# Projections of q, k, v and u interleaved, mean-square matmul issued later, and the state-space output moved to a pool of its own

## The chip, the cores and the metric

One core of a Trainium2 chip runs the kernel. The metric is device time in microseconds (us). The engines are TensorE (PE in the profile; PEld is its loading of stationary operands), VectorE (DVE), ScalarE (ACT), GpSimd (POOL) and SyncE (SP), which issues every DMA of this kernel from one queue in order. Each engine runs its own instructions strictly in the order in which they stand in its queue, and waits at an instruction whose inputs or whose destination are not ready.

## The reference, cut to what matters

One layer over 2048 tokens of 1024 features, all in float32. One projection of the normed input gives q, k, v, two SiLU gates, the state-space input u and the merge logits. Attention is differential (two softmaxes, the second weighed with -lambda), the second branch is a diagonal complex state space with GELU and a gated linear unit, and both are merged and projected out.

```python
h = rms_norm(x, norm_gain[layer])
z = h @ w_in[layer]
q, k, v, gate_a, u_s, gate_s, merge_logits = jnp.split(z, IN_SPLITS, axis=-1)
q = rms_norm(q.reshape(B, L, ATTN_HEADS, 2, ATTN_SUB_DIM), q_norm_gain[layer])
k = rms_norm(k.reshape(B, L, ATTN_HEADS, 2, ATTN_SUB_DIM), k_norm_gain[layer])
o_a = diff_attention(q, k, v, lam, rel_bias_table, diff_subln_gain[layer], lam_init)
o_a = o_a * jax.nn.silu(gate_a)
o_s = s5_branch(u_s, ...)          # y = Re(C x) + D u, x_t = lambda x_(t-1) + B u_t; GELU; GLU
o_s = o_s * jax.nn.silu(gate_s)
g = jax.nn.sigmoid((merge_logits + merge_gate_b[layer]).astype(f32)).astype(x.dtype)
merged = g_a * (o_a @ proj_attn[layer]) + g_s * (o_s @ proj_ssm[layer])
x = x + merged @ w_out[layer]
```

## The kernel before

**Precision.** Each float32 operand is split into an upper half (`hh`, `wh`, `uh`) and the rest (`hl`, `wl`). A product takes three matmuls, upper by upper, upper by lower and lower by upper (`split3`, L42 to L46). The copy that makes the upper half runs on ACT (`hilo`, L840 to L844), the subtraction on POOL or DVE.

**Stages.** The tokens are worked in four blocks of 512 (`NTB`, `TB`). `phase1` (L101) projects the normed input. `load_x` brings a block of x, scales and splits it into `hh[t]`, `hl[t]`, and computes the tokens' mean square. The weights come in groups of 256 columns (`load_w`) or tiles of 128 (`load_w1`), and are split as they arrive.

- `qk` (L207) makes 256 columns of q or k for 512 tokens: two halves of 24 matmuls each into PSUM tiles `ps_qk`, ACT squares them, DVE adds the squares. The norm is left pending: `later()` runs it (`qk_norm`, L229) behind the first half of the next block. It begins with two matmuls `ms` against a block matrix of ones (L231, L232). DVE and ACT then turn the mean square into a factor (`newton`, L90), DVE scales both halves, and each is split into `qh` and `ql` and stored to DRAM in four DMAs. `qh` and `ql` share the tag `"o"` with two buffers.
- `value` (L247) makes 256 columns of v for 128 tokens in 24 matmuls of 256 columns. Behind v's blocks 2 and 3 of a token block it also calls `later()`.
- u takes four tiles of 128 columns (L293 to L316), then come 24 tiles of gate columns (`gate`), SiLU for eight and tanh for sixteen.

The order in the program is: q group 0 with v group 4 behind each token block, then q group 1 alone, v group 5 alone, k groups 2 and 3 alone, u, then the steps of `mid()`, and the gates. The last 512 tokens of the last two gate columns (`LATE = 2`) are left to `last()`.

`mid()` holds the state space's work of small matrices and the constants of attention. `ssm_prep` (L706) computes the discretized matrices with tiny operations on DVE. In a loop of four rounds POOL makes `cp` (C times powers of lambda, L785 to L796, stored to the DRAM tensor `CD`), DVE makes `wn` and PE transposes it (`ps_w`, L810). `ssm_states` scans the chunks on DVE. `ssm_out` (L915) computes the output in 16 groups: load u, the states `x`, the matrices `w` and the Toeplitz tile `tm`, split all four, 12 matmuls of 256 columns into `ps_y`, and a GELU through ACT (Square), POOL, DVE, ACT (Tanh) and DVE.

`early()` loads the first head's K, V and Q and takes the PSUM banks for scores. Attention then runs over four heads and 16 blocks of 128 queries each: scores `ps_s` (L528, L529), maxima, exponentials and the combination of both halves on DVE and ACT, transposes `ps_t` (L560), values `ps_o` (L568). The gated linear unit (`ps_g`), the state space's projection and, at the end, the output projections (`Tail`) fill in beside it.

**What sets the order.** The program is written as one sequence. A scheduler places each instruction on its engine's queue at build time, by the order of the program and a timeline that it keeps of engines and buffers, so steps that are far apart in the text can be interleaved on an engine. Buffers come from pools in SBUF and PSUM; a pool that takes the place of a closed one waits until the instructions that used that place are done.

## Time and profile before

| | |
|---|---|
| time, median of 3 runs | 1815.27 us (1812.55 to 1816.9) |
| span of the profiled execution | 1807.6 us (7.7 us less than the median time) |
| busy share of the span | PE 94%, PEld 79%, DVE 55%, ACT 38%, POOL 18% |
| mean granted clock of TensorE | 0.979 |
| DMA | 239.06 MB, mean 132 GB/s |

The stages follow each other on PE like this, from the first and last starts of their matmuls in the trace's answers by tile:

| stage | from the span's start, us |
|---|---|
| projections of q, k and v, up to the last mean square | 7.3 to 375.6 |
| u | 358.6 to 456.6 |
| transposes of the state-space matrices (`ps_w`) | 456.6 to 509.9 |
| gates, up to the late ones; the state space's output (`ps_y`) 877.4 to 1024.9 among them | 512 to 1060.8 |
| scores and values of attention; the gated linear unit and the state space's projection among them | 1046.2 to 1576.0 |
| output projection | 1553.3 to 1800.7 |

How to read it: PE is the engine with the largest busy share, but the share is a mean over stages. In a row of idle time, the name behind the arrow is what the engine waited for. A row of a timeline gives the start, the duration, engine, line, operation, what is written and read, and in brackets the wait ahead of it. A matmul's duration in such a row includes its way through the array; the rate is read from the distance between two starts. A row of a table of stretches gives, behind the stretch's length, the busy time and the count of instructions of PE, PEld, DVE, ACT and POOL, the granted clock (1.00 is full speed), the share of the DMA engines' time and the rate.

### The profile page before, as it was taken

To read this page: it belongs to the slowest core of one execution; us is meant where nothing else is said; L and a number is where in the kernel's file an instruction comes from. 1 tells how busy PE (TensorE), PEld (TensorE's weight loads), DVE (VectorE), ACT (ScalarE), POOL (GpSimd) and SP (SyncE) were. 2 spreads that over 40 slices of the span, in tenths; PEclk is the share of its full clock that TensorE was granted. 3 is DMA by queue.
4 is the path that set the end of the run, shared out by engine and by line. 5 is a ranking of instruction groups with operands and counts; after the bars stand their busy time and mean duration, and the time that the engine had idled before them with its cause. 6 is when DMAs were issued, how large, how long until landed. Compare 5 with 4: busy or idle time off the path is not lost.

```text
span 1807.6 us, 24838 instructions
## 1 busy us (share of the span) xinstructions
PE 1701.5 (94%) x8720; PEld 1432.4 (79%) x8720; DVE 997.1 (55%) x2400; ACT 682.3 (38%) x1404; POOL 328.1 (18%) x442
## 2 busy tenths in 40 slices
PE   7879798889699999999999999999999999999999
PEld 5777786677588887887888878878888879888887
DVE  7644314469832495495223277678677678643331
ACT  5443222220123413311344366667554567511100
POOL 4331110004200000000345334553011022100000
PEclk9989899999899999999999999999999999999999
DMA  5332322233444323225656584763554543554532
GB/s 168 102 100 87 92 73 72 69 105 84 126 139 121 122 76 122 80 71 158 185 153 169 171 262 116 198 212 112 193 178 133 161 139 117 186 156 151 148 100 82
DMA packets 213005, 239.06 MB, mean 132 GB/s; under 512 B 41456, under 2 KB 151440, under 8 KB 211856
## 3 DMA queue, kind: packets, MB, share of 16 engines
q1 hardware_dynamic: 212880, 237.47, 43.5%
q8 instruction: 69, 1.13, 0.3%
q14 instruction: 56, 0.46, 0.1%
HBM read 146.44 MB, written 90.96 MB: 131 GB/s over the span
## 4 chain that ended last, share of the span: by engine, by line
PE 58%; DMA 17%; DVE 16%; ACT 3%; issue 3%; POOL 1%; SPq 1%; DVEq 0%; ACTq 0%; POOLq 0%
PE ps_p L44 8%; PE ps_p L45 8%; PE ps_p L46 8%; DMA K<-ql 5%; PE ps_o L568 5%; DVE t L879 4%; DMA Q<-ql 4%; PE ps_o L45 3%; PE ps_o L46 3%; PE ps_o L44 3%; PE ps_s L528 3%; PE ps_s L529 3%; PE ps_t L560 2%; DVE V L879 2%; PE ps_a L46 2%
## 5 line engine op out<-in xcount | busy, mean ns | idle before, releaser
L44 PE MATMUL ps_p<-hh,w 128*128 128x512 f32 x896 | 353.6, 395 | 2.4 <-DVE u L313 1.2
L45 PE MATMUL ps_p<-hl,w 128*128 128x512 f32 x896 | 353.2, 394 | 0.0
L46 PE MATMUL ps_p<-hh,w 128*128 128x512 f32 x896 | 352.7, 394 | 0.0
L44 PEld LDWEIGHTS ps_p<-hh,w 128*128 128x128 f32 x896 | 170.5, 190 | 38.0 <-DVE q L240 2.0
L46 PEld LDWEIGHTS ps_p<-hh,w 128*128 128x128 f32 x896 | 170.4, 190 | 35.3 <-issue 0.7
L45 PEld LDWEIGHTS ps_p<-hl,w 128*128 128x128 f32 x896 | 170.4, 190 | 34.5 <-issue 0.7
L541 ACT ACTIVATE e<-e,mm 128x640 f32<-128x640 f32 (+11 forms) x96 | 136.2, 1419 | 63.8 <-DVE mm L539 62.9
L568 PE MATMUL ps_o<-V,at 128*128 128x128 f32 x1088 | 148.5, 276 | 2.3 <-ACT sq L574 1.8
L568 PEld LDWEIGHTS ps_o<-V,at 128*128 128x128 f32 x1088 | 141.4, 192 | 9.3 <-ACT sq L574 2.3
L329 DVE TENSOR_TENSOR z<-ps_p,E 128x512 f32<-128x512 f32 x96 | 65.9, 686 | 132.7 <-PE ps_p L46 132.7
L531 DVE TENSOR_SCALAR_CACHE_REDUCE e<-ps_s 128x512 f32<-128x512 f32 (+1 forms) x192 | 120.6, 640 | 31.2 <-PE ps_s L529 29.7
L528 PE MATMUL ps_s<-K,Q 128*128 128x512 f32 (+3 forms) x320 | 129.0, 405 | 1.1 <-DVE e L531 0.8
L529 PE MATMUL ps_s<-K,Q 128*128 128x512 f32 (+3 forms) x320 | 115.9, 365 | 0.0
L44 PE MATMUL ps_qk<-hh,wh 128*128 128x512 f32 x256 | 101.6, 403 | 12.6 <-DVE wh L138 7.7
L45 PE MATMUL ps_qk<-hl,wh 128*128 128x512 f32 x256 | 101.2, 399 | 1.4 <-DVE hl L175 1.4
L46 PE MATMUL ps_qk<-hh,wl 128*128 128x512 f32 x256 | 101.9, 398 | 0.3 <-DVE wl L141 0.3
L335 ACT ACTIVATE z<-z,hmb 128x512 f32<-128x512 f32 x64 | 46.3, 723 | 144.6 <-DVE z L329 131.0
L560 PE MATMUL ps_t<-ident,e 128*128 128x128 f32 x544 | 85.1, 274 | 4.6 <-ACT at L562 2.5
L551 DVE SCALAR_TENSOR_TENSOR e<-e,cf 128x128 f32<-128x128 f32 (+7 forms) x64 | 88.2, 1378 | 1.4
L562 ACT COPY at<-ps_t 128x512 f32<-128x512 f32 (+3 forms) x160 | 79.3, 522 | 18.4 <-PE ps_t L560 17.8
L560 PEld LDWEIGHTS ps_t<-ident,e 128*128 128x128 f32 x544 | 66.4, 141 | 16.6 <-ACT at L562 4.2
L534 DVE CUSTOM_DVE_ANT_0 e<-ps_s,nb 128x384 f32<-128x384 f32 (+3 forms) x128 | 70.1, 552 | 16.6 <-PE ps_s L529 15.5
(334 smaller groups left out, 3464.4 us busy)
## 6 DMA issues: line engine op xcount, KB each, us to landing
wraw<-win SPq DMA_DIRECT2D x80, 256.0 KB
TM<-z SPq DMA_DIRECT2D x30, 512.0 KB
t<-TM SPq DMA_DIRECT2D x40, 256.0 KB
xs<-xT SPq DMA_DIRECT2D x32, 256.0 KB
u<-US SPq DMA_DIRECT2D x64, 128.0 KB
K<-K SPq DMA_DIRECT2D x8, 1024.0 KB
Q<-Q SPq DMA_DIRECT2D x32, 256.0 KB
Q<-Q SPq DMA_DIRECT2D x64, 128.0 KB
```

The costliest lines, as they stand in the source:

```text
L44: nc.tensor.matmul(out, wh, xh, start=start, stop=False)
L45: nc.tensor.matmul(out, wh, xl, start=False, stop=False)
L46: nc.tensor.matmul(out, wl, xh, start=False, stop=stop)
L528: nc.tensor.matmul(ps, Q[:, 0, s, 128 * b:128 * b + 128], Kt[s][:, ks], start=True, stop=False)
L529: nc.tensor.matmul(ps, Q[:, 1, s, 128 * b:128 * b + 128], Kt[s][:, ks], start=False, stop=True)
L531: nc.vector.tensor_scalar(out=et[:, ks], in0=ps, scalar1=0.0, scalar2=3e38, op0=ALU.add, op1=ALU.min, accum_out=mc[:, i:i + 1])
L541: nc.scalar.activation(out=et, in_=et, func=AF.Exp, bias=mm, scale=-1.0, accum_out=su)
L551: nc.vector.scalar_tensor_tensor(out=e[0], in0=e[1], scalar=cf, in1=e[0], op0=ALU.mult, op1=ALU.add)
L560: nc.tensor.transpose(pt[:, x], e[:, o:o + 128], k.ident)
L562: nc.scalar.copy(AT[g][:, :w], pt[:, :w])
L568: nc.tensor.matmul(po, AT[x // 4][:, x % 4], Vt[x // 8][:, x % 8], start=x == 0, stop=x == n - 1)
L879: tt = lambda o, a, b, op: eng.tensor_tensor(out=o, in0=a, in1=b, op=op)
```

## The change

**Fillers.** `qk` now takes a function `between(i)` that it calls behind each half. In the q groups 0 and 1 it issues two blocks of `value`; in the k groups 2 and 3 it issues one u tile (`state`) behind each half of token blocks 0 to 2, and both of token block 3 behind that block's second half. So v group 5 moves from behind q group 1 into it, and the four u columns from behind k into it. `later()`, with the two `ms` matmuls, now stands behind the fillers of the first half, and v's blocks no longer call it.

**u.** It takes its norms from `RT`, four tiles of `newton` made ahead of k, is written time-reversed within a chunk of eight steps, and is stored in 16 DMAs of 256 KB rather than 8 of 512 KB. Its weights take two buffers each of the tags `wh` and `wl`, which the groups of 256 columns use as well.

**PSUM.** The pool `pn` of the mean squares goes, `pF` (two banks) lives for the whole kernel and takes them, and `pm` has 6 banks rather than 5.

**Gates and hand-over.** `early`, `last`, `keep` and `LATE` go: all gate columns are finished in `phase1`, and the loads of K, V and Q for the first head are issued behind it.

**State space.** The pools of `ssm_prep` move to the other side of SBUF, under the places of the projections' pool `ep`. C, B and the temporaries share tiles. The loop for `CD` has 8 rounds of two pairs rather than 4 of four (32 stores rather than 16), `wn` is made in 8 rounds for all eight steps at once rather than step by step, and it takes `cp`'s tiles. `ssm_out` uses a pool `k.so` that is kept to the end of the kernel, loads `tm` in 2 DMAs per group rather than 8, and its tiles later serve `Tail` in place of the pools `t1` and `pm4`. The remaining differences are names and removed comments.

```diff
-LATE = 2
...
-def phase1(tc, k, I, mid, early, keep):
-    """The projections of the normed input, and steps that the last of them wait for: the gates' last columns
-    over the last tokens."""
+def phase1(tc, k, I, mid):
...
-        pm = pool("pm", 5, space=PSUM)
+        pm = pool("pm", 6, space=PSUM)
...
+        def load_w1(c, tags=("wl", "wl")):
...
-        def qk(g, t, gcol, dst, between=lambda: None):
-            """256 columns: the first and the second halves of four sub-heads' features."""
+        def qk(g, t, gcol, dst, between):
...
+                between(i)
                 if i == 0:
                     later()
-                between()
...
-            if b % 4 >= 2:
-                later()
...
+            for g in range(2):
+                if g:
+                    steps(load_w(1), 4)
+                    steps(load_w(5), 4)
+                for t in range(NTB):
+                    x = load_x(t + 1) if g == 0 and t + 1 < NTB else iter(())
+
+                    def between(i):
+                        for b in range(2 * i, 2 * i + 2):
+                            steps(x, 2)
+                            value(4 + g, 4 * t + b)
+                        steps(x, 1 + 8 * i)
+
+                    qk(g, t, k.qg, k.QT[g], between)
...
+            RT = []
             for t in range(NTB):
-                x = load_x(t + 1) if t + 1 < NTB else iter(())
-                qk(0, t, k.qg, k.QT[0], lambda: steps(x, 2))
-                for b in range(4):
-                    value(4, 4 * t + b)
-                    steps(x, 2)
-            steps(load_w(1), 4)
-            for t in range(NTB):
-                qk(1, t, k.qg, k.QT[1])
-            steps(load_w(5), 4)
-            for b in range(16):
-                value(5, b)
+                RT.append(et("x", "R"))
+                newton(nc, k, k.ep, E[:, t * TB:(t + 1) * TB], TB, RT[t], EPS ** 0.5)
...
+                w = [load_w1(16 + 2 * (g - 2) + i, ("wh", "wl")) for i in range(2)]
+
+                def state(i, t):
+
+                    u = k.wp.tile([128, 8, 64], F32, tag="wraw", bufs=2, name="u")
+                    ps = pm.tile([128, TB], F32, tag="pm", name="ps_u")
+                    proj1(w[i], t, ps)
+                    v = lambda x: x.rearrange("p (c a) -> p c a", a=8)
+                    nc.vector.tensor_tensor(out=u[:, ::-1].rearrange("p a c -> p c a"), in0=v(ps), in1=v(RT[t]), op=ALU.mult)
+                    nc.sync.dma_start(k.US[2 * (g - 2) + i][:, :, 64 * t:64 * t + 64], u)
+
                 for t in range(NTB):
-                    qk(g, t, k.kg, k.KT[g - 2])
+                    def between(i):
+                        if t < NTB - 1:
+                            state(i, t)
+                        elif i:
+                            state(0, t)
+                            state(1, t)
+
+                    qk(g, t, k.kg, k.KT[g - 2], between)
...
+        for c in cols:
...
-        w = {c: gate(c, range(NTB - 1)) for c in cols[n:]}
-
-    def last(ps):
-        for c in (*cols[-2:], *cols[n:-2]):
-            gate(c, (NTB - 1,), w[c] if c in cols[-2:] else None, ps)
-
-    return last
...
+        for a in range(0, 16, 2):
+            s = slice(a, a + 2)
+            out = [p.tile([128, 2, 9, 16], F32, tag=f"cp{i}", name=f"cp{i}") for i in range(2)]
             cmul(g, out[0], out[1], cc[0][:, s], cc[1][:, s], pj[0][:, s], pj[1][:, s], w[0], w[1], neg_im=True)
...
+        for q in range(0, 16, 2):
+            out = [p.tile([128, 2, 8, 16], F32, tag=f"cp{i}", name=f"wn{i}") for i in range(2)]
+            s = slice(q, q + 2)
+            cmul(v, out[0], out[1], cc[0][:, s], cc[1][:, s], pj[0][:, s, 0:8], pj[1][:, s, 0:8], w[0], w[1])
+            ps = k.pF.tile([128, 2, 2, 2, 64], F32, tag="F", bufs=k.NF, name="ps_w")
...
-            for tau in range(8):
-                s = slice(q, q + 4)
-                cmul(v, out[0][:, :, tau], out[1][:, :, tau], cc[0][:, s, tau], cc[1][:, s, tau],
-                     pj[0][:, s, 7 - tau], pj[1][:, s, 7 - tau], w[0][:, :, tau], w[1][:, :, tau])
...
-            for tau in range(8):
-                nc.sync.dma_start(f(tm[16 * tau:16 * tau + 16]), k.KD[:, gs, 128 - 16 * tau:256 - 16 * tau])
...
+            src = k.KD[:, 2 * a + i, 16:144]
+
+            nc.sync.dma_start(f(tm[:, i]), type(src)(src.tensor, src.offset, [[16, 8], *src.ap]))
...
+        k.NF = RINGS["F"]
+        k.pF = es0.enter_context(tc.tile_pool(name="pF", bufs=k.NF, space=PSUM, reuse_waits="tile"))
+
         def mid():
...
+            with ExitStack() as e2:
+                for _ in ssm_prep(tc, k, I, e2):
+                    pass
+                ssm_states(tc, k)
+            with ExitStack() as e2:
+                attn_consts(tc, k, I, e2)
+            k.so = es0.enter_context(tc.tile_pool(name="so", bufs=1, reuse_waits="tile"))
+            ssm_out(tc, k, k.so)
+
+        phase1(tc, k, I, mid)
         es4 = es0.enter_context(ExitStack())
-
-        def early():
-            k.heads = Heads(tc, k, es4)
-            k.heads.head(0)
-            k.heads.load_q(0, ORDER[0][0])
-            k.pS = es4.enter_context(tc.tile_pool(name="pS", bufs=RINGS["S"], space=PSUM, side="right", reuse_waits="tile"))
-
-        keep = es0.enter_context(ExitStack())
-        last = phase1(tc, k, I, mid, early, keep)
+        k.heads = Heads(tc, k, es4)
+        k.heads.head(0)
+        k.heads.load_q(0, ORDER[0][0])
...
-            last(lambda: k.pF.tile([128, TB], F32, tag="F", bufs=k.NF, name="ps_p"))
-            keep.close()```

Three places of the new order. First VectorE in the k groups: `sq` is the sum of squares, `sl` its lower half, `ms` the mean square, `ql` a stored lower half; the block before is being normed at the same time. Before:

```order
L218 TENSOR_TENSOR sq<-sq 128x512
L97 SCALAR_TENSOR_TENSOR nw_a<-nw_a,nw_y 128x512
L98 SCALAR_TENSOR_TENSOR tt<-nw_a,nw_y 128x512
L844 TENSOR_TENSOR sl<-sq,sh 128x512
L240 SCALAR_TENSOR_TENSOR q<-ps_qk,small,tt 128x512
L240 SCALAR_TENSOR_TENSOR tt<-ps_qk,small,tt 128x512
L844 TENSOR_TENSOR ql<-q,qh 128x512
L234 TENSOR_TENSOR tt<-ms,E 128x512
```

After:

```order
L214 TENSOR_TENSOR sq<-sq 128x512
L856 TENSOR_TENSOR sl<-sq,sh 128x512
L302 TENSOR_TENSOR u<-ps_u,R 128x64x8 x2
L230 TENSOR_TENSOR tt<-ms,E 128x512
L92 TENSOR_TENSOR nw_a<-nw_y,tt 128x512
L93 SCALAR_TENSOR_TENSOR nw_a<-nw_a,nw_y 128x512
L94 SCALAR_TENSOR_TENSOR tt<-nw_a,nw_y 128x512
L236 SCALAR_TENSOR_TENSOR q<-ps_qk,small,tt 128x512
L236 SCALAR_TENSOR_TENSOR tt<-ps_qk,small,tt 128x512
```

The norm of the block before no longer stands between the sum of squares and its lower half, and the scaling of u stands ahead of the reader of the mean square.

Second, TensorE where the transposes `ps_w` of the state-space matrices begin. Before, behind the last matmuls of u (`ps_p` with the tile `w_3267` and its lower half):

```order
L44 MATMUL ps_p<-hh_133,w_3267 128x512
L45 MATMUL ps_p<-hl_134,w_3267 128x512
L46 MATMUL ps_p<-hh_133,w_3268 128x512
L810 MATMUL ps_w<-ident,wn_3625 128x128
L810 MATMUL ps_w<-ident,wn_3626 128x128
```

After, among matmuls of a gate column (`w_5968`):

```order
L41 MATMUL ps_p<-hl_142,w_5968 128x512
L42 MATMUL ps_p<-hh_141,w_5969 128x512
L40 MATMUL ps_p<-hh_141,w_5968 128x512
L41 MATMUL ps_p<-hl_142,w_5968 128x512
L819 MATMUL ps_w<-ident,wn_3721 128x128
L42 MATMUL ps_p<-hh_141,w_5969 128x512
L40 MATMUL ps_p<-hh_141,w_5968 128x512
```

The transposes have moved from ahead of all gates into the gates' fifth column tile, 437 matmuls behind the first gate.

Third, TensorE where the gates hand over to the scores (`ps_s`). Before, two gate columns' last tokens stand among the first scores, and no matmul of the state space's output is left:

```order
L46 MATMUL ps_p<-hh_133,w_8323 128x512
L44 MATMUL ps_p<-hh_133,w_8322 128x512
L528 MATMUL ps_s<-K,Q 128x256
L529 MATMUL ps_s<-K,Q 128x256
L45 MATMUL ps_p<-hl_134,w_8322 128x512
L46 MATMUL ps_p<-hh_133,w_8323 128x512
L528 MATMUL ps_s<-K,Q 128x384 x2
L44 MATMUL ps_p<-hh_133,w_8322 128x512
```

After, the scores begin behind the last gate, among the state space's output (`ps_y`):

```order
L42 MATMUL ps_p<-hh_136,w_8287 128x512
L525 MATMUL ps_s<-K,Q 128x128
L526 MATMUL ps_s<-K,Q 128x128
L525 MATMUL ps_s<-K,Q 128x256
L526 MATMUL ps_s<-K,Q 128x256
L40 MATMUL ps_y<-uh,th 128x256
L41 MATMUL ps_y<-u,th 128x256
L42 MATMUL ps_y<-uh,tm 128x256
```

Of the 16 groups of `ps_y`, 16 stood ahead of the first score before; now 6 do, and 10 stand between the first score and the first `ps_g` of the gated linear unit.

208 lines of the change are left out of this document (95 added, 113 removed).

## The prediction

> **What bounds the kernel now.** I read the page first, then the table of stretches, the waits and the chain of the first 500 us, and then the attention by groups of instructions. Prices come from one profiled execution of 1807.6 us; the median of the runs is 1815.3 us, so 7.7 us lie around the span and are added at the end.
>
> ```profile
> span 1807.6 us, 24838 instructions
> PE 1701.5 (94%) x8720; PEld 1432.4 (79%) x8720; DVE 997.1 (55%) x2400; ACT 682.3 (38%) x1404; POOL 328.1 (18%) x442
> ...
> 0.00:40.00 40.00, 27.33 (x139) 21.89 (x140) 29.78 (x49) 19.63 (x34) 14.20 (x21) 1.00 0.55 164
> 40.00:360.00 320.00, 273.02 (x1444) 234.91 (x1443) 127.71 (x196) 105.86 (x197) 53.17 (x39) 0.93 0.30 87
> 360.00:457.00 97.00, 90.17 (x382) 72.85 (x380) 77.45 (x219) 15.16 (x26) 23.68 (x20) 0.96 0.34 90
> 457.00:512.00 55.00, 41.24 (x177) 33.64 (x178) 39.58 (x169) 11.26 (x24) 11.04 (x10) 0.91 0.46 136
> 512.00:1040.00 528.00, 522.59 (x2445) 434.10 (x2444) 251.66 (x558) 173.14 (x332) 76.47 (x85) 0.99 0.43 131
> 1040.00:1100.00 60.00, 57.53 (x332) 48.44 (x331) 42.12 (x139) 41.36 (x103) 20.30 (x39) 1.00 0.70 215
> 1100.00:1560.00 460.00, 446.22 (x2756) 390.45 (x2755) 342.32 (x947) 285.54 (x635) 124.84 (x219) 0.99 0.51 158
> ```
>
> The columns after the stretch are busy PE, PEld, DVE, ACT and POOL, the granted clock, the DMA share and GB/s. PE sets the end: from 512 us on it is idle for some 25 us in all. It is idle for 80 us before that, and there alone is the clock clearly under 1. Who it waits for there, and behind what:
>
> ```profile
> PE ms L231 <- ACT sh L842: 39.0, 9, 11.0
> PE ps_w L810 <- DVE wn L693: 8.7, 2, 5.3
> ...
> PE ps_w L810 <- ACT wi L814: 5.2, 1, 5.2
> ...
> 315.40 7.26 DMA K<-ql
> 323.48 7.13 DMA K<-ql
> ...
> 363.56 0.39 PE L45 MATMUL ps_p<-hl,w 128*128 128x512 f32 x1
> 363.79 0.39 PE L46 MATMUL ps_p<-hh,w 128*128 128x512 f32 x1
> 368.48 0.79 PE L231 MATMUL ms<-sh,bones 128*128 128x512 f32 x1 [4.30 <-ACT sh L842]
> ...
> 369.81 0.63 PE L45 MATMUL ps_p<-hl,w 128*128 128x512 f32 x1
> 370.24 0.63 PE L46 MATMUL ps_p<-hh,w 128*128 128x512 f32 x1
> ```
>
> The mean-square matmul stands in PE's queue ahead of projections that are ready, and waits for its input. The chain rows tell why the input is late. A normed half goes out by a store of over 7 us, and the two buffers of that ring serve both halves and both parts. So 323.48 - 315.40 = 8.1 us pass per half, 16.2 us per block of q or k, where a k block alone gives PE only 48 matmuls. The timeline shows the second cost: matmuls start 0.23 us apart before the wait, 0.43 us after it.
>
> **Term 1, the projections of q, k, v and u.** Their work is the same before and after. At 0.227 us a matmul of 512 columns and 0.12 us a matmul of 256 columns, from the starts in these rows:
>
> ```profile
> 7.35 1.19 PE L44 MATMUL ps_qk<-hh,wh 128*128 128x512 f32 x2 [7.35 <-DVE wh L138]
> ...
> 33.10 0.28 PE L253 MATMUL ps_v<-wl,hh 128*128 128x256 f32 x1
> 33.22 0.28 PE L254 MATMUL ps_v<-wh,hl 128*128 128x256 f32 x1
> ...
> L46 PE MATMUL ps_qk<-hh,wl 128*128 128x512 f32 x256 | 101.9, 398 | 0.3 <-DVE wl L141 0.3
> L254 PE MATMUL ps_v<-wh,hl 128*128 128x256 f32 x256 | 75.3, 295 | 0.0
> L810 PE MATMUL ps_w<-ident,wn x32: 270/275/476, 456.6 to 509.9; 128*128 128x128 f32 x32
> ```
>
> Three lines of 256 give 768 for q and k (174 us) and 768 for v (92 us); u has 4 x 4 x 24 = 384 (87 us); 40 mean-square matmuls are 9 us. That is 362 us. Before, the stage lasts from 7.3 us (the first matmul) to 456.6 us (the first ps_w), so 87 us are lost: waits plus the slow clock behind each.
>
> The change puts two blocks of v (5.7 us) or one of u (5.4 us) behind each half of q or k. A block then takes PE about 22 us, more than the 16.2 us of the store ring, and the mean square comes some 16 us of matmuls after its block. The longest wait, 11.0 us, stood behind one block of v (2.9 us), so its chain needs 14 us at most. DVE's new rows show the u between the lower half and the consumer of the mean square. I expect the 39 us of waits and the clock lost behind them to go. What stays: 13 us at the start (table: 12.7 us idle in the first 40 us; the first column tile now waits for all of x alone), 10 us where the next tokens' x arrives during q's first columns, and about 12 us at three weight changes, since the k groups and the u columns now fill all weight buffers and the next group can load only in the last fillers. That is 35 us lost in place of 87: **-52 us**. The ends: 20 us lost (start and one reload) and 60 us (all but k's waits stay): -67 to -27.
>
> The u stores are 16 of 256 KB in place of 8 of 512 KB; at a DMA share of 0.30 to 0.34 they have room, and I count them at nothing.
>
> **Term 2, the state-space matrices.** Before, the first ps_w stands right behind u's last block, and 457 to 512 us lose 13.8 us idle and 0.09 x 55 = 5 us of clock: 19 us. In the new order 437 rows, 99 us at the prices above, stand between the first gate and the first ps_w. But the preparation starts about 50 us of matmuls later too: its place in memory is now under the projections' buffers, so it waits for k's last norm. It also runs through a tighter loop on POOL:
>
> ```profile
> 405.91 0.18 DVE L383 TENSOR_SCALAR xa_r<-par 128x16 f32<-128x16 f32 x1
> ...
> 424.77 1.24 POOL L693 TENSOR_TENSOR bigc<-bc,P 128x576 f32<-128x576 f32 x1 [167.42 <-DVE P L693]
> ...
> 439.76 1.45 POOL L693 TENSOR_TENSOR cp<-bigc,bigc 128x576 f32<-128x576 f32 x1 [3.62 <-DMA CD<-cp]
> ...
> 464.97 1.44 POOL L693 TENSOR_TENSOR cp<-bigc,bigc 128x576 f32<-128x576 f32 x1 [11.95 <-DMA CD<-cp]
> ```
>
> The four rounds become eight of half the size, and wn now takes the places of cp, so it waits for all eight and their stores. One operation of half the size is about 0.7 us, seven are 4.6 us; with a store wait of 3.6 us a round is 8.2 us, with 12 us it is 16.6 us. DVE's preparation took 424.8 - 405.9 = 19 us to POOL's first operation; with the last norm ahead of it I set 28 us. So ps_w's input is there 28 + 66 = 94 us after the gates begin at the one end and 28 + 133 = 161 us at the other, against 99 us of cover. I take 12 us of waiting, nearer the low end, because the 11.95 us wait stood behind a u store on SP that is gone by then: **-7 us**, ends -19 and +43.
>
> **Term 3, the hand-over from gates to attention.** This is where the change gives something back. Before, all 16 groups of the state-space output run under the gates, and the last blocks of two gate columns run beside the first scores. The preparation now comes later against the same gates, and only 6 groups stand ahead of the first score; 10 run among the first 15 query blocks, ahead of the first ps_g. PE's own work in that stretch, by counting the new order: 144 score matmuls (27 us), 120 of ps_y (14 us), 174 of transposes, values and norms at 0.11 us (19 us): 61 us. DVE's:
>
> ```profile
> L531 DVE TENSOR_SCALAR_CACHE_REDUCE e<-ps_s 128x512 f32<-128x512 f32 (+1 forms) x192 | 120.6, 640 | 31.2 <-PE ps_s L529 29.7 <-PE ps_t L560 0.8
> L551 DVE SCALAR_TENSOR_TENSOR e<-e,cf 128x384 f32<-128x384 f32 (+15 forms) x62 | 87.3, 1409 | 1.4
> L534 DVE CUSTOM_DVE_ANT_0 e<-ps_s,nb 128x384 f32<-128x384 f32 (+3 forms) x126 | 69.3, 554 | 16.6 <-PE ps_s L529 15.5 <-PE ps_t L560 0.9
> L547 DVE SCALAR_TENSOR_TENSOR cf<-su,neglam,rs 128x1 f32<-128x1 f32 x62 | 18.9, 304 | 1.3
> L531 DVE DVE_READ_ACCUMULATOR e<-ps_s 128x1 f32 x192 | 15.8, 82 | 0.0
> ...
> L946 DVE TENSOR_TENSOR z<-ps_y,y 128x512 f32<-128x512 f32 x16 | 11.0, 690 | 45.9 <-POOL y L945 45.9
> L948 DVE SCALAR_TENSOR_TENSOR z<-z,ps_y 128x512 f32<-128x512 f32 x16 | 11.0, 685 | 7.2 <-ACT z L947 7.0
> ...
> L844 POOL TENSOR_TENSOR u<-u,uh 128x512 fp32r<-128x512 f32 x16 | 20.7, 1296 | 17.7 <-DMA w<-CD 12.1 <-ACT uh L842 5.6
> ```
>
> Of 318 banks of scores 69 must be out before the 72nd can start: (120.6 + 69.3 + 15.8) x 69 / 318 = 45 us. Thirteen blocks with 91 of 544 key blocks combine in 87.3 x 91 / 544 = 15 us, their small operations, of which L547 is the largest, take an estimated 13 us (1 us a block), and ten groups of ps_y 10 x 1.38 = 14 us: 87 us. So DVE, not PE, bounds this stretch. At full use it takes 87 us, at the 0.70 of the row 1040 to 1100 it takes 124 us. I take 97 us, nearer to full use, because that row's first part is PE-bound by the late gates. PE then loses 97 - 61 = 36 us where it lost 2.5 us. The first score also needs K, V and Q (3.75 MB, 17 us at the 215 GB/s of the row 1040 to 1100); they now lie over the first gates' operands and can start when the last column leaves the first tokens, 20 us of PE work ahead: hidden, 3 us for the row of waits on SP. Behind the stretch more of the fillers are left for the rest of attention, whose 13.8 us of idle should shrink by 4 us: **+33 us** in round numbers, ends +22 (87 us) and +60 (124 us).
>
> The TensorE clock bears on this term. One short wait was enough to lower it here:
>
> ```profile
> PE ps_b L430 <- ACT tbh L842: 2.4, 1, 2.4
> 840.00:860.00 20.00, 17.62 (x69) 13.12 (x68) 9.03 (x31) 3.01 (x5) 0.62 (x2) 0.91 0.50 167
> ```
>
> The Trainium skill, TensorE: Matmul & The Clock Gate, Part 1, says under "HAM oscillation" that idle gaps over about 3.4 us are what re-throttles. By that rule the 36 us, which come in pieces of about a microsecond, leave the clock full and the sum stands; the 2.4 us of this row differ from it, and the trace decides that the lower clock is a rival.
>
> **Left at nothing.** The output's Toeplitz tile loads in 2 transfers in place of 8 (96 fewer issues in all); under the gates PE is busy for 522.6 of 528 us, so that buys nothing there, and in the hand-over it keeps SP under DVE. The longer life of the output's pool and the Tail's tiles in it act in the last 250 us, where PE does not wait.
>
> **Sum.** -52 - 7 + 33 = -26 us: 1807.6 - 26 = 1781.6 us of span, **1789 us** with the 7.7 us around it.
>
> **Rivals.** (a) Nothing is given back: ten ps_y groups and the late loads hide in DVE's slack. Then term 3 is about 0: 1789 - 33 = 1756 us. For it: DVE is busy for only 42 of 60 us there now; against it: the count of 87 us against 61 us. (b) The front stays bound by x and by ACT, which waits for the store ring in its own queue, so that half of term 1 goes: 1789 + 26 = 1815 us. For it: ms waits came also among v's blocks; against it: the cover grows from three v blocks to about 16 us. (c) Slower: the ten groups lock step with attention. Each has casts on ACT, four subtractions on POOL (1.3 us for u), 12 matmuls, Square, POOL, DVE, Tanh and DVE, with one buffer for each upper half; under the gates the groups took (1024.9 - 877.4) / 15.8 = 9.3 us each:
>
> ```profile
> L44 PE MATMUL ps_y<-uh,th x32: 277/280/283, 877.4 to 1024.9; 128*128 128x256 f32 x32
> ```
>
> If every one of six hand-overs waits behind an attention instruction of about 1.2 us (the rows have 0.55 to 1.41 us), a group takes 9.3 + 7 = 16.3 us and the stretch 163 us: 1789 + 66 = 1855 us. It decides from 12.6 us a group, where the 26 us are gone (97 + 26 = 123 us, plus the measurement's 4 us). (d) Slower by the same measure on POOL: rounds of 16.6 us make ps_w wait 62 us in place of 12 us: 1839 us; from 13 us a round the gain is gone. (e) The clock halves in the hand-over: 61 us of matmuls become 115 us, over the 97 us: +18 us, 1807 us.
>
> **Chances.** Forecast 0.56, (a) 0.17, (b) 0.09, (c) 0.07, (d) 0.06, (e) 0.05. A change of 0.2% (3.6 us) is about what a measurement tells from none. Faster: nearly all of the forecast (0.52), (a) 0.17, half of (b) and (e) 0.07: 0.76. Same: 0.08 from the upper end of the forecast, (b) and (e). Slower: 0.16, from (c), (d) and the rest. The forecast's own range is 1765 to 1811 us; with (a) below and part of (b) to (d) above, 1752 to 1828 us should hold 8 in 10.
>
> **What would show it.** In the new profile: the wait of ms for sh near zero and the last u matmul at about 405 us (term 1; over 430 us it is wrong); ps_w waiting for about 12 us, with CD stores named on POOL (term 2); PE idle for 30 to 40 us between the last gate and the first ps_g, with DVE at 0.9 (term 3; under 10 us means (a), over 60 us means (c)). The prediction fails as a whole if the gates do not start before 430 us, or if ps_y or ps_w shows single waits of tens of microseconds.

## The result

The changed kernel takes 1834.61 us (median of 4 runs, 1833.1 to 1835.76) against 1815.64 us for the kernel before: a ratio of 1.011, with an interval of 1.0092 to 1.0128. The forecast was 1789 us, 26 us faster; it is 19 us slower, outside the 1752 to 1828 us that were to hold 8 in 10. Its profiled execution spans 1832.7 us, 25.1 us more than that of before. In every run that lists both, the span lies 1.7 to 1.9 us under the time of its own execution. So the profiled execution of before took about 1809 us and was some 6 us faster than the median. The 7.7 us that the prediction puts around the span are therefore about 1.8 us and that difference, and the stage table below, which compares single executions, shows about 6 us more between the kernels than the medians do.

The table of stretches of the changed kernel, cut at its own stages (columns as in the prediction: busy PE, PEld, DVE, ACT, POOL, the granted clock, DMA share, GB/s): q's first group, its second, k with u up to the first gate, the gates, first score to first `ps_g`, and the rest of attention.

```profile
span 1832.7 us, 24575 instructions
PE 1719.2 (94%) x8720; PEld 1444.9 (79%) x8720; DVE 984.5 (54%) x2268; ACT 698.0 (38%) x1418; POOL 331.2 (18%) x470
```

```profile
0.00:133.00 133.00, 110.07 (x590) 93.27 (x591) 73.68 (x131) 63.53 (x115) 47.92 (x45) 0.94 0.41 115
133.00:237.40 104.40, 96.83 (x587) 86.68 (x586) 33.35 (x44) 31.25 (x58) 13.42 (x10) 0.95 0.31 86
237.40:461.90 224.50, 190.96 (x789) 152.58 (x787) 85.44 (x118) 46.75 (x79) 5.47 (x5) 0.92 0.30 77
461.90:1037.60 575.70, 566.52 (x2577) 466.85 (x2578) 298.11 (x746) 171.29 (x315) 69.10 (x92) 0.98 0.39 121
1037.60:1137.70 100.10, 84.08 (x518) 72.58 (x516) 80.40 (x233) 84.34 (x198) 69.35 (x97) 0.91 0.72 210
1137.70:1580.60 442.90, 423.32 (x2592) 372.65 (x2590) 323.09 (x866) 266.43 (x589) 121.88 (x211) 0.98 0.53 162
```

The third row holds a surprise: 224.5 us, with the clock at 0.92, for a stage in which the mean square hardly waits any more. The waits of PE up to the first gate say what it waits for instead (what waits, what it waits for, us in total, times, the longest):

```profile
PE ps_qk L40 <- ACT wh L135: 16.2, 3, 12.1
PE ps_p L40 <- ACT w L146: 10.9, 1, 10.9
...
PE ps_u L40 <- ACT w L146: 6.1, 2, 5.4
...
PE ms L227 <- ACT sh L854: 1.2, 1, 1.2
```

The 39.0 us of waits at `ms` are down to 1.2 us, as forecast. In their place stand waits for split weights: in the k groups, at u and at the first gate.

To compare stages, take each one's length less its matmuls at full clock (0.227 us for 512 columns, 0.12 us for 256, and so on, as in the prediction). What is left is lost to waits and to the slow clock, in us, the 7.3 us ahead of the first matmul included. The first gate matmul stands at 461.7 us before (among the rows of `ps_w`, and not at 512 us, where the stage table of before lets the gates begin) and at 461.9 us after:

| stage | before | after | forecast of the difference | measured |
|---|---|---|---|---|
| q, first group (start to its end) | 45.4 | 40.2 | | |
| q, second group with v | 17.5 | 12.9 | | |
| k and u, to the first gate | 35.2 | 46.0 | | |
| **term 1**, these three | 98.1 | 99.1 | -52 | +1 |
| **term 2**, `ps_w` and the gates, to the first score | 26.2 | 19.9 | -7 | -6 |
| first score to first `ps_g` | 2.1 | 29.9 | | |
| the rest, to the end | 38.0 | 40.4 | | |
| **term 3**, these two | 40.1 | 70.3 | +33 | +30 |
| sum | 164.4 | 189.3 | -26 | +25 |

Terms 2 and 3 came out in size; term 1 did not come at all.

### The profile page after: what moved, and what is told of

Read it like the earlier page. It is cut to its first block, busy times and chain, and to the rows that moved or that the text cites. A ratio compares the mean times of both kernels' runs of the same rounds, so it can differ in the third digit from the quotient of the medians.

```text
span 1832.7 us, 24575 instructions
## 1 busy us (share of the span) xinstructions
PE 1719.2 (94%) x8720; PEld 1444.9 (79%) x8720; DVE 984.5 (54%) x2268; ACT 698.0 (38%) x1418; POOL 331.2 (18%) x470
## 3 DMA queue, kind: packets, MB, share of 16 engines
q8 instruction: 69, 1.13, 0.3%
## 4 chain that ended last, share of the span: by engine, by line
PE 56%; DMA 15%; DVE 13%; ACT 3%; issue 3%; POOL 2%; SPq 2%; DVEq 0%; POOLq 0%; ACTq 0%
PE ps_p L40 6%; PE ps_p L42 6%; PE ps_p L41 6%; DVE t L891 4%; PE ps_o L565 4%; PE ps_o L41 3%; PE ps_o L42 3%; PE ps_o L40 3%; PE ps_t L557 2%; PE ps_s L525 2%; PE ps_s L526 2%; DMA wraw<-win 2%; PE ps_qk L42 2%; PE ps_qk L41 2%; PE ps_qk L40 2%
## 5 line engine op out<-in xcount | busy, mean ns | idle before, releaser
L40 PE MATMUL ps_p<-hh,w 128*128 128x512 f32 x768 | 303.2, 395 | 10.9 <-ACT w L146 10.9
L41 PE MATMUL ps_p<-hl,w 128*128 128x512 f32 x768 | 302.7, 394 | 0.0
L42 PE MATMUL ps_p<-hh,w 128*128 128x512 f32 x768 | 301.5, 394 | 0.0
L40 PEld LDWEIGHTS ps_p<-hh,w 128*128 128x128 f32 x768 | 146.1, 190 | 41.9 <-ACT w L146 11.3
L41 PEld LDWEIGHTS ps_p<-hl,w 128*128 128x128 f32 x768 | 146.1, 190 | 30.5 <-issue 0.7
L42 PEld LDWEIGHTS ps_p<-hh,w 128*128 128x128 f32 x768 | 145.6, 190 | 30.0 <-issue 0.4
L528 DVE TENSOR_SCALAR_CACHE_REDUCE e<-ps_s 128x512 f32<-128x512 f32 (+1 forms) x192 | 120.8, 641 | 35.7 <-PE ps_s L526 31.0
L525 PE MATMUL ps_s<-K,Q 128*128 128x512 f32 (+3 forms) x320 | 130.1, 410 | 5.3 <-DVE mc L531 3.1
L40 PE MATMUL ps_qk<-hh,wh 128*128 128x512 f32 x256 | 106.2, 415 | 24.6 <-ACT wh L135 16.2
L526 PE MATMUL ps_s<-K,Q 128*128 128x512 f32 (+3 forms) x320 | 116.6, 369 | 1.4 <-DMA Q<-Q 1.4
L41 PE MATMUL ps_qk<-hl,wh 128*128 128x512 f32 x256 | 105.5, 412 | 2.1 <-DVE hl L170 2.1
L42 PE MATMUL ps_qk<-hh,wl 128*128 128x512 f32 x256 | 105.2, 411 | 1.9 <-DVE wl L136 0.9
L548 DVE SCALAR_TENSOR_TENSOR e<-e,cf 128x128 f32<-128x128 f32 (+7 forms) x64 | 97.8, 1530 | 1.4
L248 PE MATMUL ps_v<-wh,hh 128*128 128x256 f32 x256 | 77.0, 303 | 13.4 <-ACT v L252 7.0
L531 DVE CUSTOM_DVE_ANT_0 e<-ps_s,nb 128x384 f32<-128x384 f32 (+3 forms) x128 | 69.6, 552 | 24.2 <-PE ps_s L526 19.1
```

Source lines behind the costliest of these rows:

```text
L40: nc.tensor.matmul(out, wh, xh, start=start, stop=False)
L41: nc.tensor.matmul(out, wh, xl, start=False, stop=False)
L42: nc.tensor.matmul(out, wl, xh, start=False, stop=stop)
L248: nc.tensor.matmul(ps, xh, wh, start=kk == 0, stop=False)
L525: nc.tensor.matmul(ps, Q[:, 0, s, 128 * b:128 * b + 128], Kt[s][:, ks], start=True, stop=False)
L526: nc.tensor.matmul(ps, Q[:, 1, s, 128 * b:128 * b + 128], Kt[s][:, ks], start=False, stop=True)
```

## The experiments

Times are medians; each ratio is to the kernel before in the same series, where its median was 1809.7, 1811.8, 1810.8 and 1812.9 us. "Ring" below is a set of buffers that are used in turn.

### What the weights wait for

The changed kernel's trace, SP's queue (start, duration, what is issued) at the change to k's second group and at the change to the first gate:

```profile
335.77 0.55 SPq L303 DMA_DIRECT2D US<-u  x1
343.78 0.34 SPq L131 DMA_DIRECT2D wraw<-win  x1
...
451.19 0.55 SPq L303 DMA_DIRECT2D US<-u  x1
...
458.17 0.38 SPq L145 DMA_DIRECT2D wraw<-win  x1
```

And what PE has in its timeline behind them:

```profile
347.63 0.80 PE L40 MATMUL ps_qk<-hh,wh 128*128 128x512 f32 x1 [12.08 <-ACT wh L135]
348.22 0.63 PE L41 MATMUL ps_qk<-hl,wh 128*128 128x512 f32 x1
...
461.85 0.80 PE L40 MATMUL ps_p<-hh,w 128*128 128x512 f32 x1 [10.90 <-ACT w L146]
```

The raw weights are requested 8.0 and 7.0 us behind a store of u, and SP's own waits at these two places name that store:

```profile
SPq L131 <- DMA US<-u: 7.4, 1, 7.4
...
SPq L145 <- DMA US<-u: 6.4, 1, 6.4
```

In the changed kernel u's tile has the tag `wraw` with its two buffers, so the next weights cannot come before u's stores have read them. The rival was that the eight buffers of the split weights are all in use anyway. Two kernels follow: both compute u's norms in each k group, and the second alone takes the last edit shown. The first is the control for the second:

```diff
-            RT = []
-            for t in range(NTB):
-                RT.append(et("x", "R"))
...
+                RT = {}
                 for t in range(NTB):
+                    RT[t] = et("x", "R")
...
-                    u = k.wp.tile([128, 8, 64], F32, tag="wraw", bufs=2, name="u")
+                    u = et("x", "u").rearrange("p (a c) -> p a c", a=8)
```

> The changed kernel with one edit that the next kernel needs: u's norms are computed again in each k group, one token block at a time, rather than once for all four; u's tiles stay in the ring of the raw weights. It is the control. Both theories: four norms more are 4 x 2.1 us of DVE and 4 x 1.3 us of ACT in a stage where neither is full, so 1835 us, within 4 us of the changed kernel.

> As the control, but u's tiles take the two places of the x ring that the single norm leaves free, and no longer the ring of the raw weights. Theory 1, the shared ring: the weights of k's second group and of the first gate cannot be loaded before the last u stores are done (the load starts at 343.8 us, 8.0 us behind the u store of 335.8 us). Then the waits of 12.1 + 3.7 us and 10.9 us and the slow clock behind them go, 20 to 30 us: about 1810 us. Rival: the split weights' own eight buffers are all in use until the last filler, so that the loads cannot start earlier anyway. Then the waits stay and the time is within 4 us of the control, 1835 us.

The control took 1835.3 us (ratio 1.0133, 1.0115 to 1.0152), the ring of its own 1807.4 us (0.9984, 0.9971 to 0.9997): 28 us less. The loss in the k and u stage fell from 46.0 to 11.2 us, and the waits of that run up to the same point are these:

```profile
PE ps_u L40 <- ACT w L146: 7.1, 2, 6.3
...
PE ms L227 <- ACT sh L854: 1.9, 1, 1.9
PE ps_qk L40 <- ACT wh L135: 1.3, 1, 1.3
```

The wait at the first gate is gone, and of 16.2 us at k 1.3 us are left. The shared ring is shown as the cause of those, and the rival of the full weight buffers fell for them. One wait for u's first weights, 6.3 us, stays. The loss behind the first score did not shrink with it, and the state space's output still runs 102 us past the first score (1107.9 against 1006.1 us).

### What made the mean square wait before

> The kernel before with one edit: from q's second group on, the normed halves on their way to DRAM take the x ring (four buffers, idle by then) in place of the ring of two. Theory 1, the prediction's reading of the old front: the store ring makes the mean square late. Then the waits of the mean-square matmul behind 165 us (11.0 + 5.9 + 4.3 us) fall below 5 us in all and with the slow clock behind them 25 to 35 us are gained: about 1785 us. Rival: the chain of the mean square itself (ACT, DVE, ACT, DVE) is longer than the cover. Then the waits stay and the time is 1815 us.

```diff
...
-                qh, ql = et("o", "qh", F32R), et("o", "ql", F32R)
+                ring = "o" if g == 0 else "x"
+                qh, ql = et(ring, "qh", F32R), et(ring, "ql", F32R)
```

1777.2 us, ratio 0.981 (0.9782 to 0.9838): 33 us less than before, from the choice of one ring. The waits of `ms` in that run, up to the end of u:

```profile
PE ms L231 <- ACT sh L843: 24.6, 6, 6.6
```

19.3 us of these lie ahead of 165 us, where the ring is as before, so 21.2 us behind that point became 5.3 us. The loss in q's second group and k went from 52.7 to 17.1 us. For the waits behind 165 us the prediction's reading of the old front, a store ring of two, is shown; but the cure needs no fillers.

> The kernel before with the ring of four for stored halves, and with v's second group as fillers behind the halves of q's second group, the mean square behind them, as in the changed kernel; k and u stay as before, so that no group's weights fill all buffers. Theory 1, fillers help where the next weights still load ahead: the 9.8 us that the run with the ring alone still lost between 180 and 220 us fall below 2 us, and the change of weights into k costs less than 3 us: 1769 us. Rival: the change of weights into and out of the pair of groups costs what the fillers bring, 8 us or more: 1777 us.

```diff
...
+            steps(load_w(5), 4)
             for t in range(NTB):
-                qk(1, t, k.qg, k.QT[1])
-            steps(load_w(5), 4)
-            for b in range(16):
-                value(5, b)
+                qk(1, t, k.qg, k.QT[1], fill=lambda i: [value(5, 4 * t + 2 * i + j) for j in range(2)])
```

1775.2 us, ratio 0.9797 (0.9758 to 0.9835), no different from the ring alone. The second q group lost 1.1 us in place of 11.8, and k with u 17.2 in place of 5.3: k's second block waited 7.3 us at one place. The rival held, and the trace shows how. The wait names DVE's scaling `q`, which needs the norm's `nw_y` from ACT; and ACT stood at casts of weights ahead of `nw_y` in its queue, waiting for their loads:

```profile
244.08 1.23 ACT L140 CAST wh<-wraw 128x512 fp32r<-128x512 f32 x2 [11.95 <-DMA wraw<-win]
...
249.68 0.62 ACT L140 CAST wh<-wraw 128x512 fp32r<-128x512 f32 x1 [3.88 <-DMA wraw<-win]
250.21 0.62 ACT L94 ACTIVATE nw_y<-tt 128x512 f32<-128x512 f32 x1
```

> As the kernel with ring and v fillers, and in q's first group the stored halves of the first two token blocks take places in the operand tile of the last tokens, which is empty until then, those of the last the x ring. Theory 1, the same store ring makes the mean square wait in the first group too (19.3 us of waits ahead of 165 us in the run with the ring alone): these waits fall below 8 us and with the clock behind them 12 to 20 us are gained: 1752 us. Rival: there the arrival of x and ACT's work on it set the pace, so the waits stay or move to other tiles: within 4 us of the kernel with ring and v fillers.

```diff
...
+                if g == 0 and t < 2:
+                    qh, ql = hh[3][:, 4 * t + 2 * i], hh[3][:, 4 * t + 2 * i + 1]
...
```

1779.1 us, ratio 0.9824 (0.9792 to 0.9855): a miss. The first group lost 53.1 us in place of 46.0. 15.1 us of `ms` waits stayed, and 8.7 us at a value block came in. So the store ring alone does not set the pace there. The trace shows what took its place: ACT's waits for the stores of `qh` up to the end of that group went from 16.5 to 5.2 us, and its waits for blocks of x from 27.3 to 43.6 us. The longest wait of `ms` stands behind the longest of these, since `sh` comes behind `hh` in ACT's queue:

```profile
106.38 0.72 ACT L174 ACTIVATE hh<-xs,small 128x512 fp32r<-128x512 f32 x1 [10.72 <-DMA xs<-xT]
...
107.53 0.60 ACT L845 CAST sh<-sq 128x512 fp32r<-128x512 f32 x1
...
108.18 0.80 PE L232 MATMUL ms<-sh,bones 128*128 128x512 f32 x1 [9.64 <-ACT sh L845]
```

In this kernel, then, the arrival of x sets that wait, in keeping with the rival.

### Where the time behind the gates goes

> The changed kernel without the last 10 of the 16 groups of the state space's output (their loads, splits, matmuls and GELU are left out; a tile of zeros is stored in place of their results). Their matmuls are 120 x 0.12 = 14 us of PE. Theory 1, the ten groups in lock with attention make the 25 us that the hand-over gives back: the time falls by 14 + 20 us or more, to 1800 us or less, and PE's idle time between the last gate and the first matmul of the gated linear unit falls below 8 us. Rival: attention's own first blocks are bound by DVE (73 us of its work against 47 us of PE's), with or without the groups. Then PE stays idle for 20 us or more there and the time falls by the 14 us and little else, to 1817 us.

> Again the changed kernel without the last 10 groups of the state space's output. In the run with six groups the 20 stores of zeros held SP for 11.9 us (1044.7 to 1056.6 us) ahead of loads of Q that attention waited for; here the zeros are stored at the head of the output's work, under the gates. Theory 1, the ten groups make most of what the hand-over gives back: 1835 - 14 (their matmuls) - 15 or more: at most 1806 us, with a loss of about 10 us behind the last gate, as in the run without late gates. Rival, attention's first blocks by themselves: 1818 to 1822 us as in the run with the stores in the way.

The second kernel's edit:

```diff
-    for a in range(16):
+    z = tl("z", [128, 2, 256], F32)
+    nc.vector.memset(z, 0.0)
+    for a in range(6, 16):
+        for i in range(2):
+            nc.sync.dma_start(rows16(k.GD, 2 * a + i), z[:, i])
+    for a in range(6):
```

The first took 1822.2 us (1.0061, 1.0042 to 1.0079), but its 20 stores stood in SP's queue ahead of Q's loads, so it tells nothing by itself. The second took 1814.6 us (1.002, 1.0006 to 1.0034): 20 us less than the changed kernel, of which 14.4 us are the missing matmuls. The loss behind the first score went from 70.3 to 62.6 us. That is between the two expectations, and nearer to the rival: attention loses most of that time without the ten groups too. Its stretch from first score to first `ps_g`:

```profile
1040.50:1067.10 26.60, 19.75 (x100) 14.62 (x98) 20.75 (x80) 19.60 (x56) 9.89 (x22) 0.87 0.83 246
```

> The kernel before with no gate matmuls left beside the first scores (LATE = 0: all gate columns end ahead of attention); the state space's output still runs under the gates. Theory 1, attention's own first blocks leave PE short of work: the stretch behind the last gate then loses what the run with six groups lost, 15 to 25 us in waits and slow clock: 1827 to 1835 us where before has 1810. Rival: the late gates are worth nothing by themselves, and what the changed kernel loses comes with the order of its state-space output or with its later loads: within 5 us of before.

```diff
-LATE = 2
+LATE = 0
...
-        for c in (*cols[-2:], *cols[n:-2]):
+        for c in cols[n:]:
```

1824.0 us, ratio 1.0069 (1.0042 to 1.0096): 12 us more than before, and 52.4 us lost behind the first score in place of 40.1. So the late gates were worth 12 us, a little under what theory 1 asked for. Only 5 of these lie ahead of the first `ps_g`.

> The kernel before with the state-space output's Toeplitz tile loaded by 2 DMAs per group in place of 8 (u is written time-reversed for it and the powers in the other matrix with it). As predicted: under the gates PE does not wait, so nothing: within 4 us of before, 1810 us. Rival: SP's queue is where the transfers of attention's start stand behind the 96 issues saved, at 0.4 us each 38 us of SP: 5 to 15 us faster.

```diff
...
-            for tau in range(8):
-                nc.sync.dma_start(f(tm[16 * tau:16 * tau + 16]), k.KD[:, gs, 128 - 16 * tau:256 - 16 * tau])
+            for i in range(2):
+                src = k.KD[:, 2 * a + i, 16:144]
+                nc.sync.dma_start(f(tm[:, i]), type(src)(src.tensor, src.offset, [[16, 8], *src.ap]))
```

1815.3 us, ratio 1.0016 (1.0001 to 1.003). The 96 issues saved buy nothing under the gates, as predicted.

### The two halves of the change apart

> The front part of the change alone: the kernel before with v and u as fillers (u in the ring of the raw weights), the mean square behind them, and everything from the state-space matrices on as before (their pools on the old side, the output under the gates with 8 transfers per tile, late gates beside attention). Theory 1: the front as changed is worth about 5 us, since its own weight waits take up what the mean square gave, and the 25 to 32 us lost from the last gate on come with the other part: about 1805 us where before has 1810. Rival: the later state space is a consequence of the front's order itself, so the hand-over suffers here as well: 1825 us or more.

> The front alone, with u's tiles in the x ring as in the run with the ring of its own. Theory 1: the 28 us which that edit brought to the changed kernel are the front's alone, so they come here too: about 1777 us, and the changed kernel's idea would be sound with its buffers apart. Rival: what is gained ahead of the gates is lost at the matrices (ps_w with less time behind u): 1795 us or more.

The front part in the kernel before (fillers, later mean square, u in `wraw`) took 1887.5 us, ratio 1.0426 (1.0406 to 1.0447); with u in the x ring 1863.5 us (1.0289, 1.0269 to 1.031). Both forecasts were far off, and the rivals were right in direction. The ring was worth 24 us here as well. By the count of the table, the front alone lost 19 us more than before up to the first gate, 33 us more from there until the first score and the first `ps_g` had both started, and 24 us more behind. Its waits, longest first:

```profile
PE ps_w L821 <- DVE wn L704: 23.2, 2, 19.8
PE ps_qk L44 <- ACT v L256: 17.3, 5, 7.1
PE ps_qk L44 <- ACT wh L140: 16.3, 4, 11.6
PE ps_p L44 <- ACT w L151: 11.6, 1, 11.6
PE ps_s L539 <- DMA Q<-Q: 10.6, 2, 10.3
```

The longest waits say part of it: the matrices are late (23.2 us), q waits for v's copies out of PSUM (17.3 us; `pm` has five banks here, six in the change), and attention waits for Q (10.6 us): its first score comes at 1132.7 us, 50 us behind the last gate at 1082.4 us.

> The other part of the change alone: the kernel before's order of q, k, v and u, with the state-space pools on the new side, the smaller rounds, the output in its own pool with two loads per tile, and no late gates. In this order all 16 groups stand ahead of the first score again. Theory 1: u's 87 us of matmuls behind k were the cover of the state-space preparation, and moving them ahead is what pushes the output into attention's start; so here only the missing late gates cost (12 us by their own run) and the matrices gain 5 to 10 us: 1811 to 1819 us where before has 1811. Rival: the new pools and loads themselves cost the hand-over its 25 us: 1830 us or more.

1808.6 us, ratio 0.997 (0.9952 to 0.9988): a little faster than before. So the back part is not slow by itself. The two parts do not add: 77 us slower and 4 us faster alone, 19 us slower together, so the back part takes back some 50 us of what the front does to the old one. Which piece of it does was not told apart.

The first row of the `ps_y` matmuls and that of the scores (shortest, median and longest duration in ns, then the first and last start), in the changed kernel:

```profile
L40 PE MATMUL ps_y<-uh,th x32: 278/282/415, 984.3 to 1132.0; 128*128 128x256 f32 x32
...
L525 PE MATMUL ps_s<-K,Q x320: 221/417/774, 1037.6 to 1577.5; 128*128 128x512 f32 x92, 128*128 128x384 f32 x60, 128*128 128x128 f32 x4, 128*128 128x256 f32 x4
```

and in the back part alone:

```profile
L40 PE MATMUL ps_y<-uh,th x32: 281/282/386, 892.7 to 1041.8; 128*128 128x256 f32 x32
...
L514 PE MATMUL ps_s<-K,Q x320: 220/397/776, 1044.2 to 1550.6; 128*128 128x512 f32 x92, 128*128 128x384 f32 x60, 128*128 128x128 f32 x4, 128*128 128x256 f32 x4
```

With u behind k the output ends 2 us ahead of the first score; with u among k's blocks it runs 94 us past it. DVE's first operation of the preparation shows why. Before (its row stands in the prediction) it came at 405.9 us, while PE had u's matmuls until 456.6 us. In the changed kernel it comes 33.5 us behind the first gate:

```profile
478.80 0.69 DVE L856 TENSOR_TENSOR ql<-tt,qh 128x512 fp32r<-128x512 f32 x1 [7.13 <-DMA K<-ql]
...
495.35 0.17 DVE L380 TENSOR_SCALAR xa_r<-par 128x16 f32<-128x16 f32 x1
```

DVE waited for stores of K there. Before, its last wait for such a store ended at 393.9 us, with u's matmuls still to run for 63 us. u's 87 us of matmuls had been the cover of the preparation. As fillers they cover the mean square, which a second pair of buffers does as well, and the preparation now runs under gates that were to cover the output.

> The changed kernel with the u part undone: v's fillers and the later mean square in the q groups, k without fillers, u behind k as before. Theory 1: u's move alone makes the change slow, by the raw weights' ring (28 us by its own run) and by the lost cover of the preparation; without it the front keeps the 16 us that v's fillers gain in q's second group and the state-space output stands under the gates: 1795 to 1805 us. Rival: the weights of two groups at once and the hand-over without late gates cost as much whichever way u goes: 1820 us or more.

> As the run with v's fillers only, and from q's second group on the stored halves take the idle x ring of four. Theory 1: the waits of the mean square in the k groups go as they did in the kernel before with that ring: 15 to 20 us less than the run without it, 1780 us, within 8 us of the kernel before with that ring (1777 us). Rival: u's or the matrices' stage takes up what k gains: 1795 us or more.

```diff
...
-                    qk(g, t, k.kg, k.KT[g - 2], between)
+                    qk(g, t, k.kg, k.KT[g - 2], lambda i: None)
...
+        for c in range(4):
+            w = load_w1(16 + c)
...
```

Both kernels drop u's tiles from the k groups and have u's loop behind k, as before; the second has the ring of four as well. Undoing u's move alone gives 1816.1 us, ratio 1.0023 (1.0004 to 1.0042): 19 us less than the whole change, but 11 us above the upper end of theory 1. The loss behind the first score fell from 70.3 to 50.1 us, and `ms` in k, bare of fillers, waited 28.4 us, more than the 10.2 us of the kernel before. With the ring of four it is 1774.3 us, ratio 0.979 (0.9759 to 0.982), the fastest median of all, though no different from the 1777.2 and 1775.2 us of the other two. All three are about 2% faster than the kernel before (ratios 0.979 to 0.981).

> The kernel with the ring of four and v's second group as fillers, and the state-space matrices issued behind the first gate column in place of ahead of all gates, their pools as before. Theory 1, as in term 2: ps_w waits because nothing of PE's stands between u and it; 96 matmuls of 0.227 us are 22 us of cover for the 18 us that are lost between 420 and 460 us. Then these fall below 5 us: about 1762 us. Rival: the state-space output ends later against the gates and is pushed into the hand-over: 1775 us or more.

```diff
...
+        gate(cols[0], range(NTB))
         mid()
         early()
-        for c in cols[:n]:
+        for c in cols[1:n]:
             gate(c, range(NTB))
```

1793.8 us, ratio 0.990 (0.9873 to 0.9927), 19 us slower than the same kernel without it: a miss. The wait at the matrices went as theory 1 said: from the end of u to the last `ps_w` 2.3 us are lost in place of 17.9. But the first score now waits for its Q:

```profile
1014.46 0.98 PE L529 MATMUL ps_s<-K,Q 128*128 128x128 f32 x3 [7.89 <-DMA Q<-Q]
```

With that wait the stage up to the first score lost 21.0 us in place of 28.6, and the loss behind the first score rose by 22 us. The rival's reason did not come: the output's matmuls end at 995 us, 19 us ahead of the first score, where without the shift they end at 994 us, 21 us ahead. The trace shows another difference. Without the shift 48 gate matmuls stand behind the first score; with it there are none, and the last starts at 1006.2 us. In the run with `LATE = 0` their lack cost 12 us. What else makes up the 22 us, of which only some 6 lie ahead of the first `ps_g`, is open. A shift of one gate column, 22 us of matmuls, was enough to change the order of steps much later, at a price above the wait that it removed.

## Why the prediction was wrong, by its steps

**The waits for the mean square go.** Right: 39.0 to 1.2 us. The ring of stores was their cause, too, for those behind 165 us; ahead of that the arrival of x has a part in them.

**What stays in term 1, "35 us lost in place of 87".** This is the step that failed, and with 53 us it is the whole error (the span is 1832.7 us against 1781.6 us; term 2 adds 1 us to it, and term 3 takes 3 us off). 99.1 us were lost where 35 were forecast. By the table's count before lost 98.1 us, not 87: it starts at 0 and ends at the first gate, where the prediction took 7.3 to 456.6 us. The 35 us, however, hold the 7.3 us ahead of the first matmul (they are in the 13 us at the start), which the 87 us leave out; counted alike, the forecast would have been about -59 us, and further off. Of the 64 us too few, 47 are in the stages with the weight changes: 12 us were given to "three weight changes, since the k groups and the u columns now fill all weight buffers", and the two stages with these changes lost 12.9 and 46.0 us, with 6.2 and 33.2 us of waits of PE for split weights among them. The prediction looked at the wrong buffers, the split ones. The diff shows u's tile with the tag `wraw`, but the u stores were costed by their share of the DMA engines alone, without asking what waits for a store to end. 35 of the 46.0 us went with the ring of its own: 28 us of time. The other 17 us are q's first group: 23 us were set (13 at the start, 10 for x), 40.2 us were lost, and before it was 45.4 us, so the fillers hardly touch what bounds it. What bounds it in the changed kernel no run took apart.

**Rival (b), "the front stays bound by x and by ACT".** In part right: the loss of q's first group stays, and in the kernel whose first group stores its halves elsewhere ACT is shown to wait for x. Behind that group it is the shared ring, which (b) does not name.

**Term 2.** The size was right, -6 for -7 us, but by luck, since two errors cancel. The preparation began 33.5 us behind the first gate, and POOL's first operation stood 61 us behind it where 28 us were set; POOL's eight rounds took 43 us (522.7 to 565.8 us) where the forecast had 66 to 133 us, since the waits for stores of CD, put at 3.6 to 12 us a round, were 0.6 us in all:

```profile
L690 POOL TENSOR_TENSOR big<-bC,P x32: 699/704/1232, 522.7 to 563.8; 128x288 f32<-128x288 f32 x32
L690 POOL TENSOR_TENSOR cp<-big,big x16: 791/808/823, 524.3 to 565.0; 128x288 f32<-128x288 f32 x16
its engine sat idle before it (us, times) until:
  DMA CD<-cp: 0.6, 1
```

`ps_w` waited 4.9 us. Rival (d) fell.

**Term 3.** +30 for +33 us, and the stretch took 100.1 us where 97 us were forecast. The reason was right only in part, and the size came out by misses that cancel. PE's own work in the stretch is 70 us, not 61: its trace has 252 transposes, values and norms, where the prediction counted 174. So 29.9 us were lost there where 36 were set; but the rest of attention, which was to give back 4 us, lost 2.4 us more. PE was idle for 16 us of the stretch, where 30 to 40 were the sign. DVE was busy for 80 of 100 us (0.80, forecast 0.9) and ACT for 84, so neither is shown to bound it alone. Of the 30 us, 12 come from the missing late gates, which the prediction named in its heading sentence and did not price. 20 us go when u's move is undone. The ten groups' own work, to which the count of DVE gave 14 us, accounts for 8 of these: without them that much less is lost. The other 12 us or so hang on the order that u's move brings, and what carries them is open. Rival (a), nothing given back, fell with the 30 us. Rival (c), groups in lock step at 16.3 us each, fell: ten groups took about 94 us, 9.4 us each, as under the gates.

**Rival (e), the slow clock.** It came, inside term 3: the granted clock is 0.91 over the 100.1 us, 9 us of full-speed time. The longest waits of PE in that stretch are these:

```profile
PE ps_s L525 <- DVE mc L531: 2.7, 4, 1.3
PE ps_y L40 <- ACT th L854: 2.7, 1, 2.7
PE ps_y L42 <- POOL tm L856: 2.4, 1, 2.4
```

None reaches 3 us. By the rule cited in the prediction the clock should have stayed full; it did not. The same page of the Trainium skill, TensorE: Matmul & The Clock Gate, has under "A second HAM failure mode: psum-queue depth-cycling" that frequent short idles between groups of matmuls make the clock oscillate as well. This stretch is nearer to that passage than to the one that the prediction chose: the granted clock is 0.50 from 1043.3 to 1053.5 us, at waits of 2.69 and 2.42 us with four matmuls between them, and from 1115.0 to 1121.8 us, at three waits of 0.83, 0.81 and 1.13 us.

**Left at nothing.** The two loads per tile: right under the gates, by a run of their own; in the hand-over no run has them apart. The longer life of the output's pool and the Tail's tiles were not tried alone.

**The failing sign.** The prediction said that it fails as a whole if the gates do not start before 430 us. They started at 461.9 us, behind a last u matmul at 450.1 us where 405 us was the sign of term 1; with u in a ring of its own, at 428.4 us.

## What to carry to other kernels

Before work is moved ahead as a filler, ask what it has been covering where it stands: u's 87 us hid the preparation behind them, and undoing that move alone gave 19 us. For every new tile, read its tag and ask who else takes turns in that ring, and which transfer must end before the next turn: stores that held the next load for 6.4 and 7.4 us in a ring of raw weights cost 28 us, and one ring widened from two to four with buffers that lay idle gave 33 us, more than any reordering here. A filler treats a wait; look first for the buffer that makes it.

## What the runs showed of the hardware that was not expected

The clock fell to 0.91 in a stretch whose longest single wait was 2.7 us, and to 0.87 in the run without ten groups, where the longest was 2.3 us. In the changed kernel 6.8 us at a granted clock of 0.50, from 1115.0 us on, came with three waits of 0.8 to 1.1 us between 1112 and 1116 us, and with none longer. The two long waits for weights were paid twice, too: behind the 12.08 us that end at 347.63 us the granted clock is 0.50 for another 9.6 us, behind the 10.90 us that end at 461.85 us for another 4.6 us. There matmuls start 0.43 us apart (349.57, 350.00) where 0.23 us is the distance at full clock.
